# One decoder layer on one core: order of the w_in pairs, decode beside the conv branch, the first projection once for all tokens, the second as seven-product pairs

## The chip, the cores and the metric

The kernel runs on one core of one Trainium2 chip. The metric is the device time of one execution in microseconds (us), the median of three runs. Engines are called by the profile's names: PE (TensorE matmul) with PEld (its weight loads), DVE (VectorE), ACT (ScalarE), POOL (GpSimd) and SP (SyncE, which here issues the DMAs).

## What is computed

One layer of a decoder, for 1024 prompt tokens and 8 decode tokens (one from each of 8 sequences with a state): 1032 columns in all, all in float32. Cut to what matters:

```python
z = x @ w_in                       # 1024 x 7688, columns shared out to all branches
bg, cg, xv, q, k, v, og, ig, fg, ga, gb = split(z)
conv_out, sconv_new = causal_dwconv(cg * xv, sconv_buf, w_conv_mix)
ya = (bg * conv_out) @ w_proj_a                      # 512 x 1024
hm, c_new, n_new, m_new = mlstm_chunked(q, k, v, li, lf, c0, n0, m0)   # 4 heads of 256
hm = sigmoid(og) * (layernorm_per_head(hm) * mhln_g)
yb = hm @ w_proj_b                                   # 1024 x 1024
merged = sigmoid(ga) * ya + sigmoid(gb) * yb
x = layer_norm(ALPHA * x + merged @ w_mix_out, ln1_g, ln1_b)   # w_mix_out 1024 x 1024
g, u = split(causal_dwconv(x @ w_ffn_up, ffn_buf, w_ffn_conv)) # 1024 x 5632
x = layer_norm(ALPHA * x + (silu(g) * u) @ w_ffn_down, ln2_g, ln2_b)
```

For the 8 decode tokens the mLSTM is one step of the recurrence: each head's 256 x 256 state is read, scaled, given one outer product, written back and multiplied by q. "Decode" below means this.

## The kernel before

**Products.** A float32 operand is split into a high part and the rest (`split_unit` L124 for weights, `Operands.split` L155 and `Many.put` for activations: a cast on ACT, a subtraction on DVE), and each product is three matmuls: high x high, high x rest, rest x high (`mm3`, `gemm`). Activations lie with features on the partitions and tokens along the columns.

**Pairs.** `pair` (L185) multiplies a slab of 1024 x 256 weights by all 1032 columns with a seven-product scheme in place of eight: the slab and the columns are cut in two, sums and differences are formed on DVE, and each of the seven products runs over two units of 256 and 260 columns. That is 7 x 2 x 12 = 168 matmuls a pair. The seven activation operands of each unit (tiles T00 to T06 and T10 to T16, class `Operands`) are built once: operands 0 and 1 from the first half of the columns (`first`), 2 to 6 from both (`second`). The w_in pairs, the gate pairs (two 128-column blocks each, then a sigmoid, written to `sg_d` in DRAM) and the 22 pairs of the FFN go this way.

**Order of the stages.** (1) Transposes of x and its operands. (2) `conv_branch`: gate pair 0, then six pairs with `gate_math` among them; its four rows go to `hm_d[8:12]` in DRAM. (3) Four heads: pairs for K, Q and V, then `mlstm_head`, beside whose small steps stand gate pairs, numbers (1,4,5), (2,6,7), (3,8) and (9,10,11); the head's rows go to `hm_d[0:8]`. (4) For three chunks of 384, 392 and 256 tokens: `prepare` loads the chunk's 12 blocks of `hm_d` and splits them; `project` multiplies them by w_proj_a (L629 to L631, 96 matmuls) and w_proj_b (192), multiplies each result by its gate (L677, L681), adds them (L682) and splits the sum (L612, L613); `mix` multiplies by w_mix_out (192 matmuls; for the last chunk `gemm_rows`, 96 of 512 columns, L706). The weights of both projections are loaded and split again for each chunk. After each chunk come its layer norm (`norm1` L740, `back1` L759) and as much of the FFN's operands (`X1`) as its tokens allow. Decode is a generator stepped inside `project(0)`, one head at each of four slabs: each head's states come by DMA, are scaled (L822) and updated (L824), and meet PE in groups of 16 products of one output row (L830). (5) 22 FFN pairs, then w_ffn_down and the second layer norm.

**What sets the order.** A scheduler at build time fixes the order of instructions on each engine from the program order and dependences; `tc.issue_after` moves a block's priority behind a named instruction. At run time each engine executes its list in order, and the tiles' buffers are reused when their last readers are done. SP issues all DMAs of data in its own order.

## Time and profile before

| | |
|---|---|
| median of three runs | 1727.38 us (1725.61 to 1731.12) |
| the profiled execution | 1729.37 us, its span 1727.6 us |
| mean granted TensorE clock | 0.989 of full speed |
| PE / PEld busy | 1682.7 us (97%) / 1611.3 us (93%) |
| DVE / ACT / POOL busy | 1217.6 us (70%) / 840.4 us (49%) / 52.2 us (3%) |
| moved by DMA | 235.69 MB, mean 136 GB/s |

A row of the windows view holds the stretch, its length, busy time and (count of) instructions of PE, PEld, DVE, ACT and POOL, the granted clock, the DMA share and GB/s. The page gives busy time for each engine and the chain that ended last. The windows view cuts the span into stretches and gives busy time, instruction counts, the granted clock and the DMA engines' share for each. A full busy share of PE doesn't mean full speed: ends of matmuls are modelled, so a stretch's speed is read from its count of matmuls and from the distance between starts in the timeline.

### The profile page before, as it was taken

Reading aid. Unit: us, or ns where it says so; the run is one execution under the profiler, and the core shown is the slowest. Engines: PE = TensorE matmul, PEld = TensorE weight load, DVE = VectorE, ACT = ScalarE, POOL = GpSimd, SP = SyncE. Lnnn points to the kernel's source line nnn. Section 1 sums busy time; section 2 is a strip of 40 time slices with the busy share of each in tenths; the row PEclk is TensorE's granted clock in tenths of the full one; section 3 lists DMA queues with packets and bytes.
Section 4 is the critical chain, followed back from the end, with each engine's and each line's share of the span. In section 5 each row is a group of like instructions: output and inputs, shape, how many; then the busy total and the mean of one; then the engine's idle time right before and its main releaser. Section 6 shows DMA issues by size and latency. Waiting matters only on the chain.

```text
span 1727.6 us, 32408 instructions
## 1 busy us (share of the span) xinstructions
PE 1682.7 (97%) x12697; PEld 1611.3 (93%) x12697; DVE 1217.6 (70%) x2489; ACT 840.4 (49%) x1635; POOL 52.2 (3%) x97
## 2 busy tenths in 40 slices
PE   8999999999999999989899989999999999999998
PEld 6999999999999999988689879999999999888986
DVE  8966567557547657678666878778888778645676
ACT  7634336435535434545455675445454455533442
POOL 0000001001001001000000010000000000000000
PEclk9999999999999999999889999999999999999999
DMA  4321223214312313699775761322223224845763
GB/s 156 95 92 51 74 65 122 91 50 125 127 50 83 120 50 105 218 358 323 228 227 166 246 181 60 110 87 74 75 77 101 82 74 142 267 147 176 247 213 123
DMA packets 243211, 235.69 MB, mean 136 GB/s; under 512 B 22563, under 2 KB 224819, under 8 KB 242539
## 3 DMA queue, kind: packets, MB, share of 16 engines
q1 hardware_dynamic: 243059, 233.63, 42.1%
q8 instruction: 99, 1.62, 0.4%
q14 instruction: 53, 0.43, 0.1%
HBM read 184.61 MB, written 49.08 MB: 135 GB/s over the span
## 4 chain that ended last, share of the span: by engine, by line
PE 88%; DMA 5%; DVE 3%; ACT 2%; issue 1%; SPq 0%; DVEq 0%; POOL 0%; ACTq 0%; POOLq 0%
PE wp L141 34%; PE wq L141 25%; PE wq L629 3%; PE wq L630 3%; PE wq L631 3%; PE wp L631 3%; PE wp L630 3%; PE wp L629 3%; PE wp L706 2%; PE wq L706 2%; DMA WR_raw<-in_w_proj_b_dram 1%; PE pa L538 1%; PE pa L546 1%; PE pa L513 1%; ACT WS_split L130 1%
## 5 line engine op out<-in xcount | busy, mean ns | idle before, releaser
L141 PE MATMUL wp<-T_x,WS_split 128*128 128x260 f32 (+2 forms) x5016 | 657.8, 282 | 4.6 <-ACT T_x L158 2.9
L141 PEld LDWEIGHTS wp<-T_x,WS_split 128*128 128x128 f32 (+1 forms) x5016 | 615.7, 188 | 8.3 <-ACT T_x L158 3.3
L130 ACT CAST WS_split<-WR_raw 128x512 fp32r<-128x512 f32 x504 | 304.0, 613 | 457.3 <-PE wp L141 179.8
L131 DVE TENSOR_TENSOR WS_split<-WR_raw,WS_split 128x512 fp32r<-128x512 f32 x504 | 338.5, 678 | 257.2 <-ACT WS_split L130 255.5
L141 PE MATMUL wq<-T_x,WS_split 128*128 128x260 f32 (+3 forms) x3792 | 498.6, 281 | 2.7 <-ACT T_x L158 1.0
L141 PEld LDWEIGHTS wq<-T_x,WS_split 128*128 128x128 f32 (+1 forms) x3792 | 465.6, 186 | 6.1 <-ACT T_x L158 1.3
L203 ACT COPY MC_copies<-wp 128x256 f32<-128x256 f32 (+1 forms) x312 | 115.2, 369 | 93.0 <-PE wp L141 89.0
L131 DVE TENSOR_TENSOR WS_split<-XS_combo,WS_split 128x512 fp32r<-128x512 f32 (+1 forms) x54 | 36.0, 667 | 34.9 <-ACT WS_split L130 34.9
L130 ACT CAST WS_split<-XS_combo 128x512 fp32r<-128x512 f32 (+1 forms) x54 | 32.6, 608 | 34.9 <-PE wp L141 34.8
L629 PE MATMUL wq<-T_ops,WS_split 128*128 128x384 f32 (+2 forms) x128 | 43.5, 340 | 5.4 <-ACT T_ops L612 2.8
L630 PE MATMUL wq<-T_ops,WS_split 128*128 128x384 f32 (+2 forms) x128 | 42.8, 334 | 0.3 <-DVE T_ops L613 0.3
L631 PE MATMUL wp<-T_h,WS_split 128*128 128x512 f32 (+1 forms) x116 | 42.9, 370 | 0.0
L630 PE MATMUL wp<-T_h,WS_split 128*128 128x512 f32 (+1 forms) x116 | 42.9, 370 | 0.0
L631 PE MATMUL wq<-T_h,WS_split 128*128 128x512 f32 (+1 forms) x116 | 42.8, 369 | 0.0
L629 PE MATMUL wp<-T_h,WS_split 128*128 128x512 f32 (+1 forms) x116 | 42.8, 369 | 0.0
L630 PE MATMUL wq<-T_h,WS_split 128*128 128x512 f32 (+1 forms) x116 | 42.6, 367 | 0.0
L629 PE MATMUL wq<-T_h,WS_split 128*128 128x512 f32 (+1 forms) x116 | 42.6, 367 | 0.0
L631 PE MATMUL wq<-T_ops,WS_split 128*128 128x384 f32 (+2 forms) x128 | 42.2, 333 | 0.1
L729 POOL TENSOR_TENSOR rs<-rs,FX_fixed 128x1 f32<-128x1 f32 (+1 forms) x18 | 15.7, 874 | 845.9 <-DVE rs L728 835.8
L483 POOL TENSOR_TENSOR t<-t,FX_fixed 128x1 f32<-128x1 f32 (+1 forms) x36 | 22.6, 628 | 604.0 <-DVE t L482 596.4
L217 DVE TENSOR_TENSOR WR_raw<-WR_raw 128x512 f32<-128x512 f32 x52 | 35.7, 687 | 1.2
L215 DVE TENSOR_TENSOR XS_combo<-WR_raw 128x512 f32<-128x512 f32 x52 | 35.4, 681 | 0.3 <-DMA WR_raw<-in_w_in_dram 0.3
(512 smaller groups left out, 2756.9 us busy)
## 6 DMA issues: line engine op xcount, KB each, us to landing
WR_raw<-in_w_ffn_down_dram SPq DMA_DIRECT2D x27, 1024.0 KB
WR_raw<-in_w_in_dram SPq DMA_DIRECT2D x26, 1024.0 KB
WR_raw<-in_w_ffn_up_dram SPq DMA_DIRECT2D x44, 512.0 KB
WR_raw<-in_w_proj_b_dram SPq DMA_DIRECT2D x12, 1024.0 KB
WR_raw<-in_w_mix_out_dram SPq DMA_DIRECT2D x12, 1024.0 KB
T_dec<-in_state_mlstm_C_dram SPq DMA_DIRECT2D x32, 256.0 KB
out_dram<-T_dec SPq DMA_DIRECT2D x32, 256.0 KB
WR_raw<-in_w_proj_a_dram SPq DMA_DIRECT2D x12, 512.0 KB
```

The costliest lines, as they stand in the source:

```text
L130: act.copy(wh, w)
L131: vec.tensor_tensor(wl, w, wh.bitcast(F32), op=ALU.subtract)
L141: pe.matmul(ps, a[:, k, :], b[:, k, :], start=start and k == 0 and i == 0, stop=stop and k == kt - 1 and i == 2, skip_group_check=onto)
L203: act.copy(t[u], ps[u][:, :UN[u]])
L215: vec.tensor_tensor(S3, A11, A21, op=ALU.subtract)
L217: vec.tensor_tensor(A11, A21, A11, op=ALU.subtract)
L483: pool.tensor_tensor(t[:rows], t[:rows], nh[:rows], op=ALU.pow)
L513: pe.matmul(s[:, :L], kr[j][:, cs], qr[j][:, cs], start=(j == 0), stop=(j == 1))
L629: pe.matmul(ps, wh[:, i, :], xh[:, 0, :], start=s, stop=False)
L630: pe.matmul(ps, wh[:, i, :], xl[:, 0, :], start=False, stop=False)
L631: pe.matmul(ps, wl[:, i, :], xh[:, 0, :], start=False, stop=e)
L706: pe.matmul(ps[t][g], a[:, 0, cols], b[:, 0, :], start=s and i == 0, stop=e and i == 2)
```

## The change

1. **Order of the w_in pairs.** The heads come first, then `conv_branch`. `gate_math` stands after the first K pair, gate pair 0 before head 0's mLSTM. Heads 0 to 2 have two gate pairs each beside them, head 3 has three; pairs 10 and 11 follow the conv branch.
2. **Decode beside the conv branch.** The generator is stepped after each conv pair's slab load, one head at a time; its tiles are TMF, TMA, TMB, RA and RB. Its work is the same, but for `vw`, now stored head by head.
3. **First projection once.** The conv rows are loaded and split after gate pair 10, into three chunks of 344 columns; w_proj_a is loaded and split once: 8 blocks x 3 chunks x 12 = 288 matmuls of 344 columns. The results times their gates go to `ya_d` in DRAM. Beside this `hidden` loads `hm_d[0:8]` in four pieces and builds the operands XH.
4. **Second projection as four pairs** over XH: 4 x 168 matmuls of 256 and 260 columns. The results times their gates, plus `ya_d`, go to `mg_d` in DRAM.
5. **Mix.** `merged` loads a chunk from `mg_d` and splits it. `mix(0)`, `mix(1)` and `gemm_rows` no longer have a `project` between them.

The core of the diff (code that only moved, or was indented, is left out):

```diff
+CA = [(i * 344, 344) for i in range(3)]
-    SIZE = dict(QA=3104, QB=3136, RA=1032, RB=1032, TMF=2064, TMA=1032, TMB=1544)
+    SIZE = dict(QA=3104, QB=3136, RA=1032, RB=1032, TMF=2064, TMA=1040, TMB=1544)
+    ya_d = dram.tile([8, P, TOK], F32, name="ya_d")
+    mg_d = dram.tile([8, P, TOK], F32, name="mg_d")
-    def conv_branch():
+    def conv_branch(beside):
-        gate_pair(0, [UR[1], Y[1]])
+        def step():
+            with tc.issue_after(cnt["slab"].ins):
+                next(beside, None)
         for g in range(2):
-            if g == 1:
-                gate_math()
             for i in range(2):
                 m = 2 * g + i
                 pair(load_pair(w_in[0], COL_CG + m * P, COL_XV + m * P), X, rows_dst(CG, UR[i]))
+                step()
...
             pair(load_pair(w_in[0], COL_BG + 2 * g * P), X, rows_dst(*BG))
+            step()
...
+        for _ in beside:
+            pass
-    conv_branch()
+    FILL = ((1, 4), (2, 5), (3, 6), (7, 8, 9))
     for h in range(H):
...
+            if h == 0 and a == 1:
+                gate_math()
+        if h == 0:
...
+            gate_pair(0, SG)
         mlstm_head(h, qkv)
-        for i in ((1, 4, 5), (2, 6, 7), (3, 8), (9, 10, 11))[h]:
+        for i in FILL[h]:
             gate_pair(i, SG)
+    conv_branch(decode())
+    gate_pair(10, SG)
+    def merged(c, stages):
+        n, span = CH[c]
+        mg = Many(MRG[c], f"mg{c}", 8, n)
+        for i, (k, cnt_) in enumerate(mg.parts(0, 8, 2)):
+            blk, base = stages[i % len(stages)]
+            a = blk.v3(base, cnt_, n)
+            load_cols(a, mg_d[k:k + cnt_], span)
+            mg.put(k, a)
+        return mg
+    cops = [Many(q, f"conv{c}", 4, 344) for c, q in enumerate((("QA",), ("QB",), ("TMF", "TMB")))]
+    TS = Blk("TMA", "stage")
+    for k in range(4):
+        r = TS.v(0, TOK)
+        sp.dma_start(r, hm_d[8 + k])
+        for c, (lo, n) in enumerate(CA):
+            cops[c].put(k, r[:, lo:lo + n].unsqueeze(1))
+    gate_pair(11, SG)
+    XH = [Operands(u, "hid") for u in range(2)]
+    def hidden(u, off, n, a, b):
+        lo, hi = UO[u][0] + off, UO[u][1] + off
+        for t, c0 in ((a, lo), (b, hi)):
+            sp.dma_start(t, hm_d[0:8, :, c0:c0 + n].rearrange("m p t -> p m t"))
+        XH[u].first(off, a)
+        XH[u].second(off, a, b)
+    for m in range(8):
+        if m % 2 == 0:
+            wa = load_slab(w_pa[0], m * P, 256, 0, 4)
+        row = GA[m % 2]
+        sp.dma_start(row, sg_d[8 + m])
+        ua = split_unit(wa[:, :, (m % 2) * P:(m % 2 + 1) * P])
+        for c, (lo, n) in enumerate(CA):
+            ps = bank() if c == 2 else wbank(("wp", "wq")[c])
+            gemm(ps[:, :n], [ua], lambda k: cops[c].at(k))
+            vec.tensor_tensor(row[:, lo:lo + n], ps[:, :n], row[:, lo:lo + n], op=ALU.mult)
+        sp.dma_start(ya_d[m], row)
+        if m % 2 == 1:
...
+                hidden(u, off, n, MC.v3(0, 8, n), Blk("TMA", "stage").v3(0, 8, n))
+    for s in range(4):
...
+        w = load_pair(w_pb[0], s * 256)
+        for j in range(2):
+            sp.dma_start(r6[2 + j], sg_d[16 + 2 * s + j])
+            sp.dma_start(r6[4 + j], ya_d[2 * s + j])
+        pair(w, XH, rows_dst(r6[0], r6[1]))
+        for j in range(2):
+            y = r6[j]
+            vec.tensor_tensor(y, y, r6[2 + j], op=ALU.mult)
+            vec.tensor_tensor(y, y, r6[4 + j], op=ALU.add)
+            sp.dma_start(mg_d[2 * s + j], y)
-    ops = prepare(0, [(YA, i * 1024) for i in range(3)])
-    dec = decode(Blk("T04", "dec"), Blk("T05", "dec"), Blk("T06", "dec"), DQ)
-    next(dec)
-    mg = project(0, ops, Z2, dec)
+    mg = merged(0, [(SB, i * 768) for i in range(4)])
-    ops = prepare(1, [(XF, 0), (XF, 1024)])
+    mg1 = merged(1, [(Blk(q, "stage"), 0) for q in ("T14", "T15")])
     mix(0, mg, ym0)
...
-    mg = project(1, ops, Z2)
-    ops = prepare(2, [(SQ, i * 1024) for i in range(3)])
+    mg = mg1
+    mg2 = merged(2, [(S2, i * 512) for i in range(4)])
     mix(1, mg, ym1)
...
-    mg = project(2, ops, Z2)
+    mg = mg2
```

How instructions stand in the engines' lists, at three places. **First, PE where decode's products stand.** Before, at the end of the gate pairs: products of w_in (L141), decode's transposes (L788), then the first product of `project(0)` (the T_ops row); decode's products (L830) follow among the 384-column products.

```order
L141 MATMUL wp<-T_x,WS_split 128x256 x12
L141 MATMUL wp<-T_x,WS_split 128x260 x12
L788 MATMUL pa<-FX_fixed 8x128 x8
L141 MATMUL wp<-T_x,WS_split 128x256 x12
L141 MATMUL wq<-T_x,WS_split 128x256 x4
L141 MATMUL wp<-T_x,WS_split 128x260 x12
L141 MATMUL wq<-T_x,WS_split 128x256 x8
L141 MATMUL wq<-T_x,WS_split 128x260 x12
L788 MATMUL pa<-FX_fixed 8x128 x4
L629 MATMUL wp<-T_ops_8645,WS_split 128x384
```

Now, in the conv branch (line numbers are those of the changed kernel: L142 is the matmul of a pair, L646 decode's product; TMA_dec and TMB_dec hold two states each):

```order
L646 MATMUL pa<-TMB_dec,FX_fixed 1x256
L142 MATMUL wp<-T_x,WS_split 128x256 x12
L142 MATMUL wq<-T_x,WS_split 128x256 x6
L142 MATMUL wp<-T_x,WS_split 128x260 x12
L142 MATMUL wq<-T_x,WS_split 128x256 x6
L142 MATMUL wq<-T_x,WS_split 128x260 x12
L646 MATMUL pa<-TMB_dec,FX_fixed 1x256
L142 MATMUL wp<-T_x,WS_split 128x256 x3
L646 MATMUL pa<-TMA_dec,FX_fixed 1x256
L142 MATMUL wp<-T_x,WS_split 128x256 x5
L646 MATMUL pa<-TMA_dec,FX_fixed 1x256
L142 MATMUL wp<-T_x,WS_split 128x256 x4
```

Decode's products moved from among the 384-column products of `project(0)` to among the 256- and 260-column products of the conv pairs. They stand in PE's list singly, between parts of a pair's products.

**Second, DVE where the merged rows are formed.** Before, inside `project(0)`: T_mg is the split of the sum of both branches, written straight from the sum (TMF_z) in SBUF.

```order
L613 TENSOR_TENSOR T_mg_8689<-TMF_z,T_mg_8689 128x384
L681 TENSOR_TENSOR TMF_z<-wq,TMF_z 128x384
L131 TENSOR_TENSOR WS_split<-WR_raw,WS_split 128x512 x2
L677 TENSOR_TENSOR TMF_z<-wp,TMF_z 128x384
L131 TENSOR_TENSOR RA_split<-WR_raw,RA_split 128x512
L131 TENSOR_TENSOR RB_split<-WR_raw,RB_split 128x512
L682 TENSOR_TENSOR TMF_z<-TMF_z 128x384
L131 TENSOR_TENSOR WS_split<-WR_raw,WS_split 128x512
L613 TENSOR_TENSOR T_mg_8689<-TMF_z,T_mg_8689 128x384
```

Now, at the last pair of w_proj_b: RA_rows and RB_rows are that pair's two result rows (L797 times the gate, L798 plus `ya_d`), WR_raw the next raw weights, T_mg the split of a chunk loaded back from `mg_d` (T_mg_10450 of chunk 1, T_mg_10855 of chunk 2):

```order
L798 TENSOR_TENSOR RB_rows<-RB_rows,TMB_rows 128x1032
L797 TENSOR_TENSOR RA_rows<-RA_rows,TMF_rows 128x1032
L699 TENSOR_TENSOR T_mg_10450<-T_stage,T_mg_10450 128x784
L132 TENSOR_TENSOR WS_split<-WR_raw,WS_split 128x512
L798 TENSOR_TENSOR RA_rows<-RA_rows,TMA_rows 128x1032
L699 TENSOR_TENSOR T_mg_10855<-T_stage,T_mg_10855 128x512 x2
L132 TENSOR_TENSOR RB_split<-WR_raw,RB_split 128x512
L132 TENSOR_TENSOR RA_split<-WR_raw,RA_split 128x512
L699 TENSOR_TENSOR T_mg_10431<-QB_stage,T_mg_10431 128x768
```

The last rows' sums now stand between splits of weights and of later chunks, and chunk 0's last split (T_mg_10431, of blocks 6 and 7) stands behind them and behind three splits of other chunks.

**Third, PE where the FFN begins.** Before: the last mix products (L706) lead to the first FFN pair (L141 on T_x tiles), with transposes of the chunk's normed rows (L768) among them; chunk 1's transposes stand ahead of these rows, among `project(2)`.

```order
L706 MATMUL wp<-WS_split,QA_mg_10811 128x512 x2
L706 MATMUL wq<-WS_split,QA_mg_10811 128x512 x2
L905 MATMUL pa<-FX_fixed,XS_combo 128x128
L905 MATMUL pa<-FX_fixed,XS_combo 128x64
L141 MATMUL wp<-T_x_9797,WS_split 128x256 x12
L141 MATMUL wq<-T_x_9800,WS_split 128x256 x12
L768 MATMUL pa<-FX_fixed,TMA_xres 128x128 x8
L141 MATMUL wp<-T_x_10712,WS_split 128x260
L141 MATMUL wq<-T_x_10715,WS_split 128x260
```

Now (L819 the last mix, L863 transposes into a norm, L881 out of one, L943 of the FFN's cache, L142 the first FFN pair):

```order
L819 MATMUL wq<-WS_split,T_mg_10856 128x512 x3
L881 MATMUL pa<-FX_fixed,TMA_xres 128x128 x8
L863 MATMUL pa<-FX_fixed,QB_ymix_10869 128x128 x8
L881 MATMUL pa<-FX_fixed,TMB_xres 128x128 x8
L863 MATMUL pa<-FX_fixed,QB_ymix_10869 8x128 x8
L881 MATMUL pa<-FX_fixed,TMA_xres 128x8 x8
L943 MATMUL pa<-FX_fixed,XS_combo 128x128 x5
L943 MATMUL pa<-FX_fixed,XS_combo 128x64
L142 MATMUL wp<-T_x_10756,WS_split 128x256 x12
L142 MATMUL wq<-T_x_10759,WS_split 128x256 x12
L881 MATMUL pa<-FX_fixed,TMA_xres 128x128 x8
L142 MATMUL wp<-T_x_11237,WS_split 128x260
```

Chunk 1's transposes (L863 on QB_ymix and L881) moved from among the products of `project(2)` to the end of the last mix, directly ahead of the first FFN pair.

## Rows read from the trace of the kernel before

**Rows 1.** The page, parts 1 and 4: busy time by engine; the chain by engine.

```profile
PE 1682.7 (97%) x12697; PEld 1611.3 (93%) x12697; DVE 1217.6 (70%) x2489; ACT 840.4 (49%) x1635; POOL 52.2 (3%) x97
...
PE 88%; DMA 5%; DVE 3%; ACT 2%; issue 1%; SPq 0%; DVEq 0%; POOL 0%; ACTq 0%; POOLq 0%
```

**Rows 2.** Windows, five stretches: busy time and count by engine, clock, DMA share, GB/s.

```profile
1100.00:1300.00 200.00, 200.00 (x1703) 200.00 (x1703) 161.39 (x283) 99.97 (x183) 0.00 (x0) 1.00 0.27 86
910.00:940.00 30.00, 30.00 (x169) 30.00 (x168) 18.16 (x28) 13.02 (x24) 0.00 (x0) 1.00 0.53 166
1660.00:1710.00 50.00, 50.00 (x223) 40.55 (x222) 34.66 (x61) 20.42 (x37) 1.64 (x3) 1.00 0.57 198
520.00:600.00 80.00, 80.00 (x660) 79.21 (x660) 58.45 (x169) 41.57 (x91) 7.98 (x16) 1.00 0.35 110
100.00:180.00 80.00, 80.00 (x683) 79.99 (x682) 52.55 (x92) 30.09 (x62) 0.00 (x0) 1.00 0.24 78
```

**Rows 3.** Windows, same columns: from the first w_proj_a product to the FFN, and two parts.

```profile
726.00:795.00 69.00, 61.10 (x366) 54.98 (x364) 54.71 (x115) 36.11 (x60) 1.05 (x1) 0.95 1.01 340
...
835.00:889.00 54.00, 44.08 (x232) 36.23 (x231) 35.18 (x81) 22.99 (x42) 2.69 (x4) 0.81 0.56 172
...
946.00:1025.00 79.00, 70.56 (x490) 62.80 (x489) 65.77 (x139) 53.29 (x117) 5.49 (x5) 0.99 0.72 224
726.00:1025.00 299.00, 272.31 (x1651) 248.14 (x1650) 219.12 (x450) 167.08 (x320) 10.62 (x12) 0.95 0.79 253
```

**Rows 4.** Timeline of PE, 737 to 747 us: start, length, line, names, count, idle before.

```profile
737.70 1.04 PE L830 MATMUL pa<-T_dec,FX_fixed 128*1 128x256 f32 x16 [2.99 <-DVE T_dec L824]
...
739.67 0.53 PE L631 MATMUL wq<-T_ops,WS_split 128*128 128x384 f32 x1
...
743.12 0.34 PE L630 MATMUL wq<-T_ops,RA_split 128*128 128x384 f32 x1
...
746.94 0.34 PE L631 MATMUL wp<-T_ops,RB_split 128*128 128x384 f32 x1
```

**Rows 5.** Waits, 726 to 1045 us: who waited for whom, total us, times, longest us.

```profile
ACT T_mg L612 <- DVE TMF_z L682: 11.4, 7, 3.8
ACT T_ops L612 <- DMA T_xf<-hm_d: 11.1, 2, 8.4
...
PEld pa L830 <- DVE T_dec L824: 7.1, 4, 4.6
```

**Rows 6.** The chain that ended last, in order of time: start us, us, what.

```profile
733.33 7.22 DMA sg_d<-RA_sg
...
862.71 1.55 DMA hm_d<-ho
864.28 1.70 DMA T_xf<-hm_d
...
887.43 0.87 PE pa L750 x8
...
1018.00 0.82 ACT TMA_xres L764
...
1023.59 1.12 ACT T_x L158 x3
```

**Rows 7.** DVE groups, 726 to 1045 us: busy us, mean ns, idle before.

```profile
L131 DVE TENSOR_TENSOR WS_split<-WR_raw,WS_split 128x512 fp32r<-128x512 f32 x85 | 56.5, 681 | 22.7 <-ACT WS_split L130 22.6
L824 DVE SCALAR_TENSOR_TENSOR T_dec<-T_dec,FX_fixed 128x256 f32<-128x256 f32 x64 | 27.0, 470 | 5.2 <-ACT T_dec L822 5.2
```

**Rows 8.** DVE group of the whole span, one of 1032 columns.

```profile
L941 DVE TENSOR_TENSOR QA_xf<-QA_xf 128x1032 f32<-128x1032 f32 x11 | 13.6, 1232 | 1.7 <-ACT QA_xf L939 1.7
```

**Rows 9.** ACT groups, 726 to 1045 us: the split of a loaded stage.

```profile
L612 ACT CAST T_ops<-T_xf 128x784 fp32r<-128x784 f32 x6 | 5.1, 842 | 12.9 <-DMA T_xf<-hm_d 11.1 <-PE wp L631 1.9
```

More of the change, by code (lines that the diff above doesn't have):

```diff
@@ L385, in trunk_kernel @@
     PT = v1(PT_B, 100)
-    CVA, CVB = Blk("QA", "conv"), Blk("QB", "conv")
     def load_params():
-        p1 = CVB.v(2064, P, 100)
+        PB = TOK
+        p1 = GB_[4].v(PB, P, 100)
         sp.dma_start(p1[0:12, :], w_conv.rearrange("o j (m c) -> (o j m) c", c=P))
@@ L490, in head_finish @@
         sp.dma_start(hm_d[2 * h:2 * h + 2, :, cols].rearrange("j p t -> p j t"), ho)
-    for i in range(2):
-        pool.memset(TV.v(VX_T[i] + 256, 2).bitcast(F32), 1.0)
-        pool.memset(TV.v(VX_T[i] + 514, 2).bitcast(F32), 0.0)
     def mlstm_head(h, qkv):
@@ L577, in trunk_kernel @@
                 vec.tensor_copy(DV[:, a, 2 * h + j, :], qkv[a][j][:, T:])
+            if h == 0 and a == 1:
+                gate_math()
+        if h == 0:
+            TA = Blk("TMF", "mlstm")
+            TV, TK = Blk("TMB", "mlstm", F32R), Blk("TMA", "mlstm", F32R)
+            for i in range(2):
+                pool.memset(TV.v(VX_T[i] + 256, 2).bitcast(F32), 1.0)
+                pool.memset(TV.v(VX_T[i] + 514, 2).bitcast(F32), 0.0)
+            SG = [Blk(q, "sg").v(0, TOK) for q in ("RA", "RB")]
+            gate_pair(0, SG)
@@ L583, in trunk_kernel @@
+    conv_branch(decode())
+    SG = [Blk(q, "sg").v(0, TOK) for q in ("RA", "RB")]
+    gate_pair(10, SG)
     class Many:
@@ L656, in load_slab @@
         return t
-    def project(c, ops, zb, beside=()):
-        beside = iter(beside)
+    def merged(c, stages):
         n, span = CH[c]
         mg = Many(MRG[c], f"mg{c}", 8, n)
-        for s in range(4):
-            wa = load_slab(w_pa[0], s * 256, 256, 0, 4)
-            wb = load_slab(w_pb[0], s * 256, 256, 0, 8)
-            with tc.issue_after(cnt["slab"].ins):
-                next(beside, None)
-            for j in range(2):
-                m = 2 * s + j
-                blk, base = zb[m % len(zb)]
-                sa, sb = (blk.v3(base + i * n, 1, n) for i in range(2))
-                load_cols(sa, sg_d[8 + m:9 + m], span)
-                load_cols(sb, sg_d[16 + m:17 + m], span)
-                cols = slice(j * P, (j + 1) * P)
-                ua = split_unit(wa[:, :, cols])
-                ps = next_bank()
-                gemm(ps[:, :n], [ua], lambda k: ops.at(8 + k))
-                vec.tensor_tensor(sa[:, 0, :], ps[:, :n], sa[:, 0, :], op=ALU.mult)
-                ub = [split_unit(wb[:, 4 * i:4 * i + 4, cols]) for i in range(2)]
-                ps = next_bank()
-                gemm(ps[:, :n], ub, lambda k: ops.at(k))
-                vec.tensor_tensor(sb[:, 0, :], ps[:, :n], sb[:, 0, :], op=ALU.mult)
-                vec.tensor_tensor(sa, sa, sb, op=ALU.add)
-                mg.put(m, sa)
-        for _ in beside:
-            pass
-        return mg
@@ new lines, in trunk_kernel @@
+    gate_pair(11, SG)
[6 more added lines that the diff above has]
+        XH[u].second(off, a, b)
+    GA = [Blk(q, "ga").v(0, TOK) for q in ("RA", "RB")]
+    for m in range(8):
[10 more added lines that the diff above has]
+        if m % 2 == 1:
+            i = m // 2
+            if i == 1:
+                t15 = Blk("T15", "stage")
+                hidden(0, P, P, t15.v3(0, 8, P), t15.v3(D, 8, P))
+            else:
+                u, off, n = ((0, 0, P), None, (1, 0, 130), (1, 130, 130))[i]
+                hidden(u, off, n, MC.v3(0, 8, n), Blk("TMA", "stage").v3(0, 8, n))
```

166 lines of the change are left out of this document (79 added, 87 removed).

## The prediction

> **What bounds the kernel now.** I read the page first: PE is busy 97% of the span and holds 88% of the chain that ended last [rows 1]. So the time changes by PE work removed, by PE idle time, and by time at the lower of its two clock levels (1.2 and 2.4 GHz). What PE pays per matmul is next, from windows in which it never stopped at full clock [rows 2]. The reader should divide length by count: pairs of 256 and 260 columns 200/1703 = 0.1174 us; 392 columns 30/169 = 0.1775; 512 columns 50/223 = 0.224. For 384 columns the timeline has 22 starts in 746.94 - 743.12, or 0.1736 each [rows 4]. None shows 344 columns: between 258 at 0.1174 and 384 at 0.1736 a straight line gives 0.1558, an estimate; the two ends are its bounds.
>
> Then the windows by stage [rows 3]. From the first w_proj_a product (726) to the first FFN pair (1025) 299 us pass, and PE is far from dense: clock 0.81 at the end of decode, 8 us idle in the last part. What dense PE work is in it? Projections 96 x 3 matmuls by (0.1736 + 0.1775 + 0.1174) = 134.9 us; mix(0) 192 x 0.1736 = 33.3; mix(1) 192 x 0.1775 = 34.1; last mix 96 x 0.224 = 21.5; some 144 transposes by 0.87/8 [rows 6] = 15.7; decode 8 groups by 1.04 [rows 4] = 8.3. Sum 247.8. So **51.2 us are lost** to idle time and low clock. The waits say to whom [rows 5]: decode's products wait for its state updates, the next chunk's split for its load (8.4 us once), the merged sums' splits for DVE. The first part's DMA engines are busy throughout (share 1.01, 340 GB/s) [rows 3].
>
> **The change, part by part.**
>
> *Projections.* Before 134.9 us. After, 288 x 0.1558 = 44.9 for w_proj_a and 672 x 0.1174 = 78.9 for the four pairs: 123.8, **11.1 us less**. With the bounds of the 344-column price it is between 22 less and 6 less. The rows price a matmul nearly by its columns; a rule speaks against that. The Trainium skill's "TensorE: Matmul & The Clock Gate", section "Back-to-back issue gap", gives a sustained spacing of about 81 ns at 128 columns and 131 at 512; a straight line between these makes narrow products dear, and by it the projections would cost some 94 us before and 97 after, 3 more. The trace disagrees: 0.224 us at 512 [rows 2].
>
> *Weights split once.* w_proj_a and w_proj_b are loaded and split once instead of three times. Before, DVE made 3 x 8 and 3 x 16 subtractions of 512 columns for them; after, 8, and in four pairs 28 more and 16 sums of weights. 20 steps of 0.68 us [rows 7] go, 13.6 us of DVE. This lay beside PE; its worth is in the losses below.
>
> *Order of the w_in pairs.* The same pairs stand there. What could be lost is the cover of a head's mLSTM, now two gate pairs for heads 0 to 2. Head 2 had two before, and PE was dense beside it: 80.00 of 80 us, full clock [rows 2]. I cost it at nothing; the cover is those pairs, and had it been short, a head would show PE gaps. `gate_math` and parameters come earlier on DVE and POOL, beside K and Q pairs; nothing too.
>
> *Decode beside conv pairs.* PE takes the same 8.3 us for its products. The 51 lost us contained its waits; the question is what it loses now. Its 64 updates of 0.47 us [rows 7] are 30 us of DVE work. The conv pairs' own load is 52.55 of 80 us [rows 2]; over the seven pairs and decode, 7 x 168 x 0.1174 + 8.3 = 146 us, that is 96 + 30 = 126 us, 86%. So DVE fits, but tightly, and PE executes its list in order: a decode product that waits for L824 holds all pair products behind it. The DMA traffic that crowded the first part is now spread over six pairs (share there 0.24 without decode [rows 2]). Bounds: nothing, or 8 groups each as bad as the rival below, 51 us. I take 3 us, near the lower end, since a state has a whole pair (19.7 us) to arrive and each product stands singly.
>
> *w_proj_a stage and XH.* PE has 44.9 us. DVE has 55 subtractions of some 512 columns by 0.68 [rows 7] and 24 multiplications of 344 columns by 0.46 (an estimate, 344/512 of 0.68): 48.7 us, of which the last part can run beside the first pair, whose operands 0 and 1 come first. Hence a loss of 0 to 8; I take 3.
>
> *Pair to mix(0).* New serial chain: last product, addition, times gate, plus ya (1.23 us each per row [rows 8]), store to and load from DRAM (1.55 + 1.70 us for small pieces, 7.22 for one transfer in the crowded part [rows 6]), cast 0.84 [rows 9] and subtraction about 0.97. DVE's order puts about nine other steps, 8 us, among them. Against it mix(0) has only 62 products, 10.8 us, that don't need the last two blocks. Also on SP the stores of the last rows stand behind loads of other chunks. Loss 4 to 13; I take 6.
>
> *Mix to mix.* mix(0) to mix(1): operands of chunk 1 are loaded beside mix(0); 1 to 6, I take 3.
>
> *Norms to the FFN.* Before, `project(2)` covered chunk 1's norms, and that part still idled 8 us [rows 3]. Now they stand beside the last mix: PE has 21.5 us of products and some 8 of transposes, DVE has, in order, five tiles of norm (3.3 us each, four 512-wide steps by 0.68 and small ones), two `second` (18 steps by 0.68 = 12.4), firsts 2.7 and 16 weight splits 10.9: 42.6 us. DVE then exceeds PE by some 13 us, and the serial end (normalise, transpose, scale, split, before from 1018.00 to 1024.7 [rows 6]) adds 7. Loss 12 to 30; I take **20**.
>
> *Sum.* New losses 3 + 3 + 6 + 3 + 20 = 35 against 51.2, so 16.2 less; with 11.1 that is 27.3. The profiled execution is 1729.4 us (span 1727.6), which gives 1702.1; the median of the runs lies 2.0 lower, so **1700 us**.
>
> **Rivals.**
>
> *Denser than I think.* With each new loss near its lower bound (0 + 0 + 4 + 1 + 12 = 17) another 18 us go: 1682. For it: the pairs have been dense everywhere [rows 2]. Against: 42.6 us of DVE beside 29.5 of PE.
>
> *The norms become the bound.* With losses at the upper bounds (the decode term at 3: 3 + 8 + 13 + 6 + 26 = 56) the whole saving of idle time is gone and only part of the PE work pays: 1700 + 21 = 1721. For it: the weights of the last mix and its splits share DVE with the norms.
>
> *Decode stalls the conv pairs, slower than before.* Place: the 8 groups of products in PE's list among the conv pairs. Price: the longest such wait was 4.6 us [rows 5]; after an idle stretch of 2.99 us starts lay 0.31 us apart (739.67 to 743.12, 11 starts) where they later lay 0.1736 apart [rows 4], so the clock's lower level costs another 1.8. Eight groups by 6.4 us are 51 us in place of 3: 1700 + 48 = 1748. It decides from about 4.5 us a group (36 us), when the forecast's 27 us are used up. For it: DVE at 86%, in order. Against: each state has a pair's time.
>
> *The idle time is only moved.* XH's operands wait for four loads of eight rows each, behind the loads of gates and weights on SP (such a wait was 8.4 us once [rows 5]). If they come late enough that two thirds of the 16.2 us return, 11 us, the time is 1711. For it: XH's operands are built from the last piece on just ahead of the pairs. Against: DVE and SP have the whole w_proj_a stage, 44.9 us, for it.
>
> *Narrow products are dear.* If matmuls in the projections cost the same whatever their columns, each costs 134.9/864 = 0.156 us, and the 960 after cost 149.9: 15 more instead of 11 less, 1700 + 26 = 1726. The pitches of 258 and 512 columns, 0.1174 and 0.224 [rows 2], speak against it. The Trainium skill's page named above, "TensorE: Matmul & The Clock Gate" ("Back-to-back issue gap"), points this way.
>
> **How the numbers follow.** Forecast 1700: 0.57. Denser, 1682: 0.20. Norms as the bound, 1721: 0.12. Decode stalls, 1748: 0.06. Idle moved, 1711: 0.04. Narrow products dear, 1726: 0.01. The forecast's own range from its terms is about 1690 to 1711. The range takes in the denser case with the best price of 344 columns (another 10 us: 1672) and the norm case (1721, with 2 for the scatter of runs: 1723); outside lie the stalls and thin tails of the two ends. A measurement of this kernel tells about 0.3% (5.2 us) from no change. Slower by more: the stall case and 0.01 of the norm case's tail, 0.07. Within 0.3% (1722.2 to 1732.6): 0.05 of the norm case, whose price lies at that border, and the dear narrow products, 0.06. Faster: the rest, 0.87.
>
> **What the changed profile would show.** PE work: the pitch at 344 columns near 0.156 us, four w_proj_b pairs of 20 us. Conv pairs with decode: a clock of 1.00 and less than 5 us of PE idle. At the turn from the last pair to mix(0): PE waits for the split of `mg_d` rows, some 6 us. Before the FFN: PE idle some 20 us, ended by the X1 splits on ACT and DVE. I am wrong if decode's products wait for L824's like several us a group, if heads 0 to 2 show PE gaps, or if the end before the FFN is dense.

## The result: 1.7% slower

The changed kernel takes 1758.51 us (median of 4 runs, 1757.52 to 1760.1) where the kernel before takes 1729.25: a ratio of **1.0172, 95% interval 1.0150 to 1.0195**. The forecast was 1700, the range 1672 to 1723. The profiled execution has a span of 1757.3 us, 29.7 more than before.

The page of the changed kernel, parts 1 and 4, against [rows 1]: PE has 10 us more busy time, and on the chain it gave up one hundredth of the span, while DVE gained two.

```profile
PE 1693.0 (96%) x12793; PEld 1621.4 (92%) x12793; DVE 1234.1 (70%) x2490; ACT 833.5 (47%) x1640; POOL 46.8 (3%) x97
...
PE 87%; DVE 5%; DMA 5%; ACT 1%; issue 1%; SPq 0%; POOL 0%; DVEq 0%; POOLq 0%; ACTq 0%
```

Where the 29.7 us are is read from stages. The w_proj_a products began at 726.4 us before and begin at 756.6 now, 30.2 later (nine of them stand ahead of that, at 749.5, among the last gate pair's). From there to the first product of the first FFN pair's second unit, the one of 260 columns (1023.1 before, 1045.3 now), 288.7 us pass instead of 296.7, where the forecast wanted some 39 less. From that product to the end it is 7.5 us longer, though not one line of that part was changed.

The windows of the changed kernel, as in [rows 3]: w_proj_a products, the gap behind them, the four w_proj_b pairs, mix(0), mix(1), last mix and norms, all of it; then a piece of the FFN for [rows 2].

```profile
756.64:802.70 46.06, 45.05 (x281) 43.75 (x279) 36.74 (x65) 19.41 (x33) 0.00 (x0) 1.00 0.89 288
802.70:813.53 10.83, 0.00 (x1) 0.03 (x1) 5.77 (x10) 3.56 (x6) 0.00 (x0) 0.60 1.05 398
813.53:896.49 82.96, 82.90 (x673) 82.69 (x673) 53.75 (x86) 30.63 (x64) 0.00 (x0) 0.97 0.58 198
896.49:939.35 42.86, 35.32 (x194) 34.97 (x193) 23.77 (x32) 18.38 (x33) 0.00 (x0) 0.92 0.66 212
939.35:979.58 40.23, 40.23 (x249) 40.03 (x247) 22.54 (x43) 28.39 (x61) 2.41 (x3) 1.00 0.58 187
979.58:1045.34 65.76, 40.58 (x194) 33.13 (x192) 42.65 (x84) 37.71 (x84) 3.08 (x5) 0.74 0.48 137
756.64:1045.34 288.70, 244.08 (x1583) 234.61 (x1581) 185.21 (x317) 138.08 (x278) 5.50 (x8) 0.91 0.64 207
```

```profile
1100.00:1300.00 200.00, 200.00 (x1676) 200.00 (x1675) 160.39 (x280) 98.27 (x180) 0.00 (x0) 1.00 0.27 85
```

Dense work in the 288.7 us, by the prediction's prices, is 43.5 (279 products of 344 columns) + 78.9 + 33.3 + 34.1 + 21.5 and 12.2 for transposes: 223.5. So some 65 us are lost there, to idle time and low clock; before it was 48.9 up to the same product (296.7 - 247.8), and the forecast had 32 without decode. By row: 2.6 in the w_proj_a products, 10.8 in the gap, 4 in the pairs, 9.6 in mix(0), 1 in mix(1), and **37 in the last row**, with a mean clock of 0.74; PE is idle for 25.2 of these (65.76 - 40.58). The FFN row has 1676 matmuls in 200 us at full clock; [rows 2] had 1703 in the same time. PE is as busy and yet slower.

Who kept PE waiting there (engine, line waited for, total us, times, longest):

```profile
PE pa L881 <- ACT TMA_xres L877: 13.0, 2, 7.9
PE wp L142 <- DVE RA_ga L772: 10.9, 1, 10.9
PE wq L715 <- ACT RA_split L131: 7.5, 1, 7.5
PE pa L881 <- ACT TMB_xres L877: 5.1, 1, 5.1
PE pa L943 <- DMA XS_combo<-in_cache_ffn_conv_dram: 3.8, 1, 3.8
PE wp L142 <- ACT T_x L159: 3.2, 1, 3.2
```

L881 are the transposes out of a layer norm, and L877 is ACT's normalisation. These two waits and the last two rows make up the idle time of the last row; 3.8 us of it are no norm, but the load of the FFN's cache (L943). The second row is the gap ahead of the pairs. It names a multiplication of the last w_proj_a blocks (L772), which must free the product's PSUM bank; the weight load of the same product is put down to the split of XH (ACT T_hid, L159), 11.1 us. The chain that ended last has the load of XH's last piece ahead of both (start us, us, what):

```profile
797.53 10.21 DMA MC_copies<-hm_d
```

That load was issued when the piece before it had left the buffer (DVE's last split of it, L160, ended at 796.3) and three other issues of SP were through, and it took 10.2 us to land. The splits it feeds stand ahead of L772 in DVE's list. The third row is mix(0): its second block's weights were to be split into the spare slot RA, which still held a row being stored to `mg_d`.

### The profile page after: what moved, and what is told of

Read it like the earlier page. It is cut to its first block, busy times and chain, and to the rows that moved or that the text cites. A ratio compares the mean times of both kernels' runs of the same rounds, so it can differ in the third digit from the quotient of the medians.

```text
span 1757.3 us, 32559 instructions
## 1 busy us (share of the span) xinstructions
PE 1693.0 (96%) x12793; PEld 1621.4 (92%) x12793; DVE 1234.1 (70%) x2490; ACT 833.5 (47%) x1640; POOL 46.8 (3%) x97
## 4 chain that ended last, share of the span: by engine, by line
PE 87%; DVE 5%; DMA 5%; ACT 1%; issue 1%; SPq 0%; POOL 0%; DVEq 0%; POOLq 0%; ACTq 0%
PE wp L142 35%; PE wq L142 27%; PE wq L715 2%; PE wq L716 2%; PE wq L717 2%; PE wp L715 2%; PE wp L717 2%; PE wp L716 2%; PE wp L819 2%; PE wq L819 2%; PE pa L540 1%; PE pa L548 1%; DMA MC_copies<-hm_d 1%; PE pa L515 1%; PE pa L646 1%
## 5 line engine op out<-in xcount | busy, mean ns | idle before, releaser
L142 PE MATMUL wp<-T_x,WS_split 128*128 128x260 f32 (+2 forms) x5016 | 668.9, 285 | 4.7 <-ACT T_x L159 3.2
L142 PEld LDWEIGHTS wp<-T_x,WS_split 128*128 128x128 f32 (+1 forms) x5016 | 624.5, 188 | 15.1 <-issue 5.7
L142 PE MATMUL wq<-T_x,WS_split 128*128 128x260 f32 (+3 forms) x3792 | 504.3, 283 | 2.4 <-ACT T_x L159 0.7
L131 ACT CAST WS_split<-WR_raw 128x512 fp32r<-128x512 f32 x486 | 294.6, 612 | 443.6 <-PE wp L142 182.8
L132 DVE TENSOR_TENSOR WS_split<-WR_raw,WS_split 128x512 fp32r<-128x512 f32 x486 | 327.4, 679 | 247.3 <-ACT WS_split L131 243.5
L142 PEld LDWEIGHTS wq<-T_x,WS_split 128*128 128x128 f32 (+1 forms) x3792 | 471.6, 187 | 6.8 <-ACT T_x L159 0.9
L204 ACT COPY MC_copies<-wp 128x256 f32<-128x256 f32 (+1 forms) x336 | 123.8, 369 | 110.3 <-PE wp L142 104.7
L142 PE MATMUL wp<-T_hid,WS_split 128*128 128x260 f32 (+1 forms) x384 | 51.0, 287 | 10.9 <-DVE RA_ga L772 10.9
L142 PEld LDWEIGHTS wp<-T_hid,WS_split 128*128 128x128 f32 x384 | 48.6, 193 | 11.4 <-ACT T_hid L159 11.1
L218 DVE TENSOR_TENSOR WR_raw<-WR_raw 128x512 f32<-128x512 f32 x56 | 38.5, 688 | 1.2
L142 PE MATMUL wq<-T_hid,WS_split 128*128 128x256 f32 (+1 forms) x288 | 38.8, 287 | 0.0
L217 DVE TENSOR_TENSOR WR_raw<-WR_raw 128x512 f32<-128x512 f32 x56 | 38.3, 683 | 0.3
```

Of the source, the lines that this page charges most:

```text
L131: act.copy(wh, w)
L132: vec.tensor_tensor(wl, w, wh.bitcast(F32), op=ALU.subtract)
L142: pe.matmul(ps, a[:, k, :], b[:, k, :], start=start and k == 0 and i == 0, stop=stop and k == kt - 1 and i == 2, skip_group_check=onto)
L204: act.copy(t[u], ps[u][:, :UN[u]])
L217: vec.tensor_tensor(A21, A21, A22, op=ALU.add)
L218: vec.tensor_tensor(A11, A21, A11, op=ALU.subtract)
```

## The experiments

The first two theories after the result: **(P)** the same products cost more because the operand tiles lie elsewhere in SBUF (TMA grew by 8 columns, since XH's pieces of 8 x 130 columns pass through it, and pushed them); **(C)** between chunk 1's mix and the FFN runs a chain of norms that takes its time whatever PE does, and the change took away the work that stood beside it. Against C: the prediction's own reading, that DVE's work or PE's is the bound there.

### e1: the kernel before, tiles 32 bytes further

```diff
-    SIZE = dict(QA=3104, QB=3136, RA=1032, RB=1032, TMF=2064, TMA=1032, TMB=1544)
+    SIZE = dict(QA=3104, QB=3136, RA=1032, RB=1032, TMF=2064, TMA=1040, TMB=1544)
```

> The kernel before with one number changed: tile TMA is 1040 instead of 1032 columns, so that every tile allocated behind it (TMB and the operand tiles T00 to T16) lies 32 bytes further in SBUF. The order of instructions on every engine is the same as before. Address theory: products of 256 columns, 12 of which took 1.36 us before and 1.43 after the change, cost what they cost by where their operands lie; so the pairs of the FFN go from 19.95 to about 20.25 us each, as in the changed kernel, and 52 pairs by 0.30 make the time some 15 us longer, about 1744. Rival (the slower pairs come from what runs beside them or from the changed order): no change, 1729 within 5, pairs of 19.95 us.

Measured: 1746.92 us, ratio 1.0099 (1.0079 to 1.0119). P holds, its rival is out. The stores of FFN rows give the length of a pair: 11 stores, 20 pairs apart from first to last. Kernel before, changed kernel, e1 (line, engine, tile, count, duration, first and last start):

```profile
L942 SPq DMA_DIRECT2D h_d<-QA_xf x11: 332/338/339, 1063.5 to 1457.1; - x11
```

```profile
L980 SPq DMA_DIRECT2D h_d<-QA_xf x11: 333/339/339, 1085.0 to 1484.7; - x11
```

```profile
L942 SPq DMA_DIRECT2D h_d<-QA_xf x11: 332/339/339, 1071.6 to 1471.6; - x11
```

That is 19.68 us a pair before, 19.98 after the change, 20.00 in e1. (The expectations say 19.95 and 20.25: they count the last, longer step too.) Within a pair it is mostly the products of 256 columns. Before, starts lie 1.36 us apart for 12 of 256 columns and 1.45 for 12 of 260; in e1 it is 1.42 and 1.44. Timelines of before and of e1:

```profile
1221.61 1.52 PE L141 MATMUL wq<-T_x,WS_split 128*128 128x256 f32 x12
1222.97 1.62 PE L141 MATMUL wp<-T_x,WS_split 128*128 128x260 f32 x12
1224.42 1.61 PE L141 MATMUL wq<-T_x,WS_split 128*128 128x260 f32 x12
```

```profile
1212.25 1.58 PE L141 MATMUL wq<-T_x,WS_split 128*128 128x256 f32 x12
1213.67 1.61 PE L141 MATMUL wp<-T_x,WS_split 128*128 128x260 f32 x12
1215.11 1.60 PE L141 MATMUL wq<-T_x,WS_split 128*128 128x260 f32 x12
```

### e2, e6, e13: the tiles of the changed kernel moved on

Only TMB's size differs (1552, 1568, 1600 for 1544):

```diff
-    SIZE = dict(QA=3104, QB=3136, RA=1032, RB=1032, TMF=2064, TMA=1040, TMB=1544)
+    SIZE = dict(QA=3104, QB=3136, RA=1032, RB=1032, TMF=2064, TMA=1040, TMB=1600)
```

> The changed kernel with TMB 8 columns longer (1552), so that the operand tiles T00 to T16 lie 64 bytes, not 32, behind where they lay before the change. Order on every engine as in the changed kernel. Address theory: FFN pairs back at about 19.95 us, 56 pairs by 0.30: about 17 us less, 1742. Rival (order, or what runs beside): 1758 within 5, pairs of 20.25.

> The changed kernel with TMB 24 columns longer (1568), so that the operand tiles T00 to T16 begin at 96 modulo 128 bytes in SBUF, as in the kernel before (the changed kernel has 0, the run with 8 columns more had 32). Order on every engine unchanged. Address theory, now by the place within 128 bytes: 12 products of 256 columns back at 1.36 us, FFN pairs at 19.95 us, 17 us less, about 1741. Rival (the address counts in another way, or the one slow shift of the kernel before was something else): 1758 to 1761.

> The changed kernel with TMB 56 columns longer (1600), so that the operand tiles begin at 96 modulo 256 bytes, as in the kernel before; e6 had them at 96 modulo 128 only (224 modulo 256) and won 9 us. Order unchanged. Address theory: 12 products of 256 columns in 1.36 us, FFN pairs of 19.95 us, 56 pairs by 0.30: 15 to 20 us less than the changed kernel's 1758.5, a ratio to before of 1.005 to 1.009. Rival (in the changed kernel the pairs are slower for another reason too): a ratio of 1.012 or more, as e6.

Measured: e2 1.0177 (1.0161 to 1.0193), nothing won; e6 1.0122 (1.0101 to 1.0142), half; e13 **1.0100** (1.0076 to 1.0124), 12 us less than the changed kernel and between what its two sides expected. e2 missed: a shift by 64 bytes in all doesn't put things back. A shift by 256 bytes in all does, as e13's row shows (19.68 us a pair):

```profile
L980 SPq DMA_DIRECT2D h_d<-QA_xf x11: 332/338/339, 1079.5 to 1473.0; - x11
```

So some 12 to 17 of the 29 us have nothing to do with the order or the products of the change. They come from 8 more columns of a buffer. In e13 the w_proj_a products begin 7.2 us earlier than in the changed kernel, and the part from the FFN's first product of 260 columns (at 1039.6) to the end is 7.5 us shorter; between the two, where PE waits anyway, nothing was won (1.4 us longer).

### e3: norms written one tile ahead

```diff
     n3 = norm1(ym1, 0, 3)
+    n4 = norm1(ym1, P, 4)
...
     back1(n3, x3, 3 * P)
+    n5 = norm1(ym1, 2 * P, 5)
...
-    for t in (4, 5):
-        back1(norm1(ym1, (t - 3) * P, t), tile_dst(MC), t * P)
-        X1[1].first((t - 4) * P, tile_dst(MC))
-    back1(norm1(ym1, 384, None), XS8, T)
+    back1(n4, tile_dst(MC), 4 * P)
+    X1[1].first(0, tile_dst(MC))
+    n8 = norm1(ym1, 384, None)
+    back1(n5, tile_dst(MC), 5 * P)
+    X1[1].first(P, tile_dst(MC))
+    back1(n8, XS8, T)
```

> The changed kernel with chunk 1's layer norms written one tile ahead: the transposes into the norm of tile t+1 stand before the transposes out of tile t. Same work. Serial-chain theory (each tile's chain of transposes, DVE, POOL, ACT, transposes, ACT, some 8.7 us, runs alone because PE's list has the next tile's transposes behind it): two to three of the five chains overlap, the stretch from the last mix product (999) to the first FFN product of unit 1 (1055) gets 15 to 25 us shorter, 1733 to 1744. Rival (DVE's 42.6 us of work in order is the bound, as the prediction had it): under 5 us less, 1754 or more.

Measured: 1.0146 (1.0123 to 1.0170), 4 us less, with intervals that overlap. The window from mix(1)'s last result to the FFN's first product of 260 columns (the 1055 of the expectation is a later product; the changed kernel has that one at 1045.3):

```profile
985.60:1042.40 56.80, 38.85 (x186) 30.74 (x184) 39.15 (x81) 35.98 (x82) 3.29 (x5) 0.78 0.54 152
```

The changed kernel takes 64.7 there (980.6 to 1045.3). So the order is worth 8 us where it was meant to work, half of the 15 that the theory asked for at the least; mix(1) ended 5 us later in e3, which takes most of it back. The rival named the right size, but its reason, DVE, isn't the bound either: in the changed kernel DVE is busy 42.65 of the last row's 65.76 us. The chain of the changed kernel shows what the time consists of (start us, us, what):

```profile
999.12 0.45 PE pa L881 x4
999.59 0.93 ACT T_xf L887 x3
1000.64 1.87 ACT T_xf L887 x5
1002.52 6.62 DMA x_d<-T_xf
1009.17 0.69 DVE T_xf L174
1010.10 0.91 POOL rs L842
1011.22 0.82 ACT TMA_xres L877
1012.09 1.97 PE pa L881 x8
1014.06 0.87 PE pa L863 x4
1014.95 0.70 DVE TMB_xres L865
```

A tile is transposed on PE (L881), scaled on ACT (L887) and stored to `x1_d` (6.62 us to landing), and until the store is through, DVE (L174) may not overwrite it with the differences that make X1; the next tile goes through POOL, ACT and PE again. Up to 999 the last mix's products run beside the norms; in the 46 us behind them no engine is full, and each step waits for the one before. Which link of the chain sets its length was not tried: no run took away the store or gave the norms another buffer.

### e5: the last mix's products issued twice

```diff
+            n = 2 if kt == 8 else 1
-            for i, (a, b) in enumerate(((xh, wh), (xl, wh), (xh, wl))):
+            for i, (a, b) in enumerate(((xh, wh), (xl, wh), (xh, wl)) * n):
```

> The changed kernel with each of the last mix's 96 products of 512 columns issued twice (that chunk's mix comes out doubled), 21.5 us more of PE work and nothing else. Cover theory (from the end of chunk 1's mix to the FFN a chain of norms, stores and loads runs for about 76 us, in the kernel before as after, and PE only waits for it; the change took project(2)'s 33.8 us of products away from beside it): the first FFN product of unit 1 stays where it is, under 6 us longer, 1758 to 1764. Rival (the norms and the products compete, PE or DVE is the bound there): 15 to 22 us longer, 1773 to 1780.

Measured: 1.0184 (1.0164 to 1.0204) beside 1.0172: 21.5 us of products for 2 us of time, within the intervals for none. The FFN's first product of 260 columns in e5, and the window from mix(1)'s last result to it:

```profile
1046.09 0.39 PE L142 MATMUL wp<-T_x,WS_split 128*128 128x260 f32 x1 [3.60 <-ACT T_x L159]
```

```profile
979.50:1046.10 66.60, 56.96 (x285) 46.52 (x283) 41.89 (x84) 37.08 (x83) 3.36 (x5) 0.95 0.45 130
```

The stretch takes 66.6 us beside the changed kernel's 64.7, though PE's busy time in it goes from 40 to 57. C holds: PE had the room. It isn't quite "nothing else" that changed: the build put the norms' transposes among the doubled products (the first of each tile's way out at 995.8, 1008.7 and 1021.7, in the changed kernel at 999.0, 1012.1 and 1020.9), so e5 doesn't say that PE's order is without effect.

### e14: the kernel before without project(2)

```diff
+                if c == 2:
+                    mg.put(m, sa)
+                    continue
                 cols = slice(j * P, (j + 1) * P)
                 ua = split_unit(wa[:, :, cols])
...
-    ops = prepare(2, [(SQ, i * 1024) for i in range(3)])
+    ops = None
```

> The kernel before without project(2): the last chunk's merged rows are its gates of branch A as loaded, so 288 products of 256 columns (33.8 us), their weights' loads and splits and the chunk's operands are left out. Cover theory (a chain of some 76 us from the end of chunk 1's mix to the FFN is what PE waits for; project(2) only ran beside it): the chain loses some load on DVE and ACT but stays over 55 us, and the kernel gets under 15 us shorter, 1715 to 1729. Rival (PE's products set this stretch before the change): 30 us or more shorter, under 1700.

Measured: 0.9920 (0.9901 to 0.9939), 14 us less, at the edge of what C said and half of what the rival did. The FFN's first product of 260 columns in e14, and the window from mix(1)'s last result to it; the same window before:

```profile
1008.41 0.59 PE L141 MATMUL wp<-T_x,WS_split 128*128 128x260 f32 x1 [2.64 <-ACT T_x L158]
```

```profile
947.90:1008.40 60.50, 40.58 (x191) 33.37 (x189) 38.41 (x78) 35.85 (x79) 3.24 (x5) 0.77 0.47 136
```

```profile
947.20:1023.10 75.90, 68.53 (x478) 61.12 (x477) 62.67 (x133) 50.33 (x111) 5.49 (x5) 1.00 0.72 225
```

With project(2) the stretch takes 75.9 us and PE is busy for 68.5; without it 60.5, and PE for 40.6. So of its 33.8 us of products 18 were free. (With them went 24 us of work on DVE and 14 on ACT, so the 15.4 that the stretch got shorter aren't PE's alone.) In the changed kernel, which has none of them, the stretch takes 64.7. C holds here in a weaker form: the chain does get longer by what runs beside it, but by less than half of it.

### e4 and e7: the gap ahead of the w_proj_b pairs

```diff
-        if m % 2 == 1:
-            i = m // 2
+        if m < 4:
+            i = m
```

> The changed kernel with the four pieces of the hidden operands XH loaded and split beside the first four of the eight w_proj_a blocks instead of beside blocks 1, 3, 5 and 7. Same work. Serial-load theory (the 10.9 us of PE idle time ahead of the first w_proj_b pair and the low clock behind it come from the last piece's load, which waits for its buffers and then for DRAM): the idle time falls to under 3 us, 8 to 13 us less, 1745 to 1750. Rival (DVE with 48.7 us of work beside 46 us of products is the bound): the idle time moves in among the w_proj_a products, under 4 us less.

Measured: 1.0179 (1.0156 to 1.0201), nothing won. But the loads did not move: the last piece's was issued at 798.9 us, beside 797.5 in the changed kernel, and took 10.65 us, since each piece goes through the two buffers of the piece before it. So e4 leaves the serial-load theory untested, and the changed kernel's own chain speaks for it. e7 takes bytes away:

```diff
-        sp.dma_start(row, sg_d[8 + m])
-            vec.tensor_tensor(row[:, lo:lo + n], ps[:, :n], row[:, lo:lo + n], op=ALU.mult)
+            vec.tensor_copy(row[:, lo:lo + n], ps[:, :n])
```

> The changed kernel without the gates of branch A: the eight rows of sg_d are not loaded beside the w_proj_a products and the results are copied instead of multiplied. 4.2 of about 16.6 MB that move in that stage go; PE's and ACT's work and DVE's count of steps stay. Transfer theory (XH's pieces come late because the DMA engines are full there, share 0.92 at 292 GB/s): the idle time ahead of the first w_proj_b pair falls from 10.9 to under 4 us, 7 to 14 us less, 1745 to 1751. Rival (the serial steps of the last piece, or DVE, are the bound): under 4 us less.

Measured: 1.0129 (1.0106 to 1.0151), 7 us less. The first pair starts at once, and the wait behind it is 1.75 us in place of 10.9. Timeline, and the last piece's load on the chain:

```profile
800.61 1.58 PE L142 MATMUL wp<-T_hid,WS_split 128*128 128x256 f32 x12
803.93 0.39 PE L142 MATMUL wp<-T_hid,WS_split 128*128 128x260 f32 x1 [1.75 <-ACT T_hid L159]
```

```profile
797.90 5.33 DMA MC_copies<-hm_d
```

The load is issued as late as in the changed kernel, and lands in half the time. So the full DMA engines have a share in the gap; its row above says so too (DMA share 1.05, 398 GB/s). But the edit did a second thing: the copy that frees the product's PSUM bank now stands ahead of the last piece's splits in DVE's list (801.3, the splits at 803.9), where L772 stood behind them (812.9, from 808.4 on). How the gap divides between the late issue, the slow transfer and the place of L772 is not shown.

### e8 to e10: parts 1 and 2 alone

e8 puts the projections of the kernel before (prepare, project, mix by chunk, tiles at their old place) behind the changed conv branch:

```diff
+    FILL = ((1, 4), (2, 5), (3, 6), (7, 8, 9))
+    conv_branch(decode())
+    gate_pair(10, SG)
+    gate_pair(11, SG)
...
-    next(dec)
-    mg = project(0, ops, Z2, dec)
+    mg = project(0, ops, Z2)
```

> Parts 1 and 2 of the change alone: order of the w_in pairs and decode beside the conv branch, with the projections chunk by chunk as before (and the operand tiles at 96 modulo 128 bytes, as before). Theory (decode's stalls made 25 us or more of the 43 us lost between 726 and 889, and beside the conv pairs they are gone but for 6 us of products that stand singly): 1705 to 1720. Rival (project(0)'s loads keep the DMA engines full with or without decode): 1727 to 1736.

Measured: 1712.69 us, **0.9883 (0.9866 to 0.9900)**, faster than both kernels, and the best of all runs. Parts 3 to 5, with the place that they brought, turn a gain of 1.2% into a loss of 1.7% (of 1.0% at the old place, e13). The window from the first projection product to the FFN's first of 260 columns:

```profile
748.66:1005.72 257.06, 246.35 (x1497) 236.69 (x1495) 174.86 (x325) 139.81 (x278) 7.76 (x8) 1.00 0.67 210
```

Without decode's 8.3 us the dense work of [rows 3] is 239.5, so 17.6 us are lost here where before it was 48.9. Parts 1 and 2 were not run apart.

The products of decode stand singly in part in the second half of each head. A product shows as two records: the x16 of [rows 4] are eight products, not sixteen. Timeline of the changed kernel:

```profile
594.40 0.59 PE L646 MATMUL pa<-TMB_dec,FX_fixed 128*1 128x256 f32 x2
594.92 0.62 PE L142 MATMUL wp<-T_x,WS_split 128*128 128x256 f32 x3
595.47 0.59 PE L646 MATMUL pa<-TMA_dec,FX_fixed 128*1 128x256 f32 x2
595.99 0.86 PE L142 MATMUL wp<-T_x,WS_split 128*128 128x256 f32 x5
```

One single product takes 0.52 us to the next start; the eight of a first half take 0.97 together (587.50 to 588.47), and so do the five or six that are left of a second half (0.96). Three halves with three singles and one with two cost some 6 us more than four groups of eight. e9 puts them together (the two loops behind this line follow it):

```diff
-                first = product(0, 3)
+                first = product(0, 3 if half == 0 else 2)
```

> Parts 1 and 2 of the change alone (the run e8), and the second half of each head's decode products headed by state 2 instead of state 3, so that its eight products stand together in PE's list. Same work. Theory (a product that stands singly takes 0.52 us from start to the next start, eight together 0.97; four halves have three such singles): 1.5 us a half, 6 us less than e8, a ratio to before lower by 0.0035 (e8 0.9883). Rival (the singles cost no more, what is lost there is waiting for states, and it comes back as a wait of the whole group): within 2 us of e8.

Measured: 0.9922 (0.9903 to 0.9942), 7 us more than e8, not 6 less. Eight do take 0.98 us (593.64 to 594.62), but PE then waits elsewhere, from 550 to 745 us:

```profile
PE wq L141 <- DVE RA_sg L199: 4.0, 1, 4.0
PE wp L141 <- ACT MC_copies L203: 2.1, 4, 1.1
PE pa L643 <- DVE TMB_dec L637: 1.4, 1, 1.4
```

In the same stretch e8 had 1.2 us of waits. The price of a single product was right; that it could be had back was not.

> The run e8 (projections by chunk as before) with chunk 1's norms written one tile ahead, as in e3. Theory (with project(2) beside it the chain of norms is mostly covered, and its length is set by buffers and by stores and loads of normed rows, not by the order of its transposes): within 5 us of e8. Rival (order of transposes matters where the cover is long enough to overlap tiles): 6 us or more less than e8.

e10 (e3's edit on e8): 0.9934 (0.9915 to 0.9953), 9 us more than e8. Neither side expected it longer. Its trace has the loss between the first projection product and the FFN's first of 260 columns (746.6 to 1012.6, 266.0 us beside e8's 257.1); the cause stays open.

### e11, e12: two more places

Edits: TMB=1560 and TMB=1600 in e9.

> The run e9 with TMB 16 columns longer: the operand tiles begin at 160 modulo 256 bytes in SBUF (before and e9: 96; the changed kernel: 0; e2: 32; e6: 224). Order unchanged. Address theory: the time of pairs changes with the place; the places seen gave 12 products of 256 columns in 1.36 us (96) and 1.42 to 1.44 (0, 32, 224), so 0 to 17 us longer than e9, or, if this place is better than any seen, a few us shorter. Rival (96 is not special, what differs between the runs was something else): within 3 us of e9.

> The run e9 with TMB 56 columns longer: the operand tiles begin at 64 modulo 256 bytes. As for e11: 0 to 17 us longer than e9 or a few us shorter by the address theory, within 3 us of e9 by the rival.

Measured: 1.0001 (0.9990 to 1.0012) and 0.9973 (0.9959 to 0.9986), 14 and 9 us more than e9. In these two only the operand tiles moved.

The places follow from the diffs. By bytes further than in the kernel before, modulo 256, a pair of the FFN takes, read as in e1's rows: 0 (before, e9, e13) 19.68 us; 32 (e1, changed kernel) 19.98 to 20.00; 64 (e2, e11) 20.04 and 20.05; 128 (e6) 19.86; 224 (e12) 19.88. In the expectations' count, which puts the kernel before at 96, these are 96, 128, 160, 224 and 64; e11's has the changed kernel at 0 and e2 at 32, which is the count modulo 128. So e11 tried a place that e2 had tried already, in another order of instructions, and the pairs agree. Which rule makes the times stays open.

## Why the prediction was wrong

**The step that failed is the cover of the norms**: "DVE then exceeds PE by some 13 us, and the serial end ... adds 7. Loss 12 to 30; I take **20**." Measured 37, above the upper bound (24 products of the first FFN pair, 2.8 us, are counted as lost in it, as they were in the 51.2 of before). The work on DVE was sized well (42.6 us forecast, 42.65 busy). But a sum of work bounds a stretch from below only. These steps form a chain over PE, DVE, POOL, ACT and DRAM, with two row buffers and one staging tile, and 60.5 us pass with only the last mix beside it (e14); 21.5 us more of products beside it made it 1.9 longer (e5). Its length stood in the trace of before: from mix(1)'s last result to the FFN, 75.9 us, of which the prediction read only that PE idled 8. The right question was how long the chain would be without project(2). The case "the norms become the bound" had the place and not the size.

**What no term had: the place of the tiles.** "The same pairs stand there. ... I cost it at nothing" and 78.9 us for four pairs rest on 0.1174 us a product from [rows 2]. In the changed kernel a pair costs 0.30 us more, 56 times: 17 us by the rows; e13 won 12 in the median and 13 in the profiled execution, since pairs among waits win nothing. The line of the diff that does it was read and passed over. The Trainium skill's "TensorE: Matmul & The Clock Gate" ("Back-to-back issue gap"), which the prediction weighed as a rival, has narrow products dear for their columns. They did get dearer here, but by their place: at the old place (e13) the price is that of [rows 2], which the page's figures don't give.

**XH, "a loss of 0 to 8; I take 3"**: 10.8 in the gap, 4 more in the pairs behind it, and 2.6 in the products, 17 in all. The bound was worked out for PE and DVE. The DMA engines were left out, though the stage loads XH and gates and stores `ya_d`, and though the same stretch of [rows 3] had shown a share of 1.01; e7 shows that they have a part in it. The rival "The idle time is only moved" had this: XH's operands late behind loads, some 11 us. At a chance of 0.04 it was priced too low.

**Pair to mix(0), 6**: measured 9.6, within its bounds, by another wait than named (the spare weight slot). **Mix to mix, 3**: 1. **344 columns, 0.1558**: starts in a dense stretch lie 0.159 apart (28 steps from 780.83 to 785.28), a little dearer.

**Decode, 3 us**: no wait for L640's updates shows on PE in the conv branch, so the rival of 1748 did not come, although the time did. That 1748 lies near the measured time is chance. (Its 1.8 us for the low clock comes out of [rows 4] as 1.5.) The products cost 6 more for standing singly, which the forecast had counted as a help. What it undervalued is the gain: without decode, the projections by chunk lose 17.6 us in place of 48.9, and e8 is 21 us faster than before. Had parts 1 and 2 been costed apart from 3 to 5, the forecast would have had a faster half and a slower one.

**Order of the w_in pairs, nothing**: in e8, with the tiles at their old place, the projections begin 22.3 us later than before (726.4, 748.7). Decode's products make 14 of it; some 8 more lie in the head and conv stages, and no run shows their cause.

**The seven-product saving, 11.1 us**, shows in part: 46.1 + 83.0 and 1.4 for the nine products ahead, 130.5 us elapsed against 134.9 of dense work before, low clock and dearer products included; the gap of 10.8 takes more than that back.

In sum, against the forecast's 1702 for the profiled execution (57 us): norms 17, place of tiles 13, XH 13 (17 less its share of the place and the 3 forecast), turn to mix(0) and mix(1) 2, decode's singles 3; the rest, some 9, is about what e8 leaves open in the head and conv stages.
